# A hybrid DeltaNet/HGRN block on one core: gates and HGRN values projected token-major, head norms taken token-major

## The chip, the cores and the metric

The kernel runs as one program on one core of a Trainium2 chip. The time is device microseconds of one execution; the time before is 1231.27 us, the median of three runs (1229.66 to 1232.65). TensorE (PE) multiplies, VectorE (DVE), ScalarE (ACT) and GpSimd (POOL) do the elementwise work, SyncE (SP) and POOL issue the transfers. Each engine takes its instructions strictly in the order in which they stand in the program; which order that is, a scheduler settles when the program is built, from its own estimates of durations.

## What is computed

One layer: a normed input (256 tokens, 2048 wide) goes through one wide projection into two groups of eight heads of 128, then an output projection, a squared-ReLU feed-forward pair and a final norm, all in float32.

```
n = RMSNorm(h)
[q k v z a b | q f i g] = n @ W_in
y_A = head_norm(gated_delta(silu(conv(q, k, v)), a, b)) * silu(z)        # 8 heads, "GDN"
y_B = head_norm(hgrn2(silu(q), f, i)) * silu(g)                          # 8 heads, "HGRN"
h = h + concat(y_A, y_B) @ W_out
h = h + relu(RMSNorm(h) @ W1)^2 @ W2
out = RMSNorm(h)
```

`head_norm(o)` divides each head's 128 outputs of a token by their root mean square and multiplies by a weight of 128 entries. The delta rule inside a chunk asks for the inverse of a triangular matrix; HGRN multiplies keys and queries by exponentials of summed log gates.

## The kernel before

**Number format.** Every large float32 operand is split into two parts, `hi` (rounded, one ACT cast, L120) and `lo` (the rest, one DVE subtraction, L121), and the product is made of three terms: hi*hi, hi*lo, lo*hi. The input is stored once, transposed, as `xT`, 16 tiles k of 128 channels by 512 columns: 256 of `hi`, then 256 of `lo`.

**Projection (`project`, L286-L328).** Weights arrive as tiles `w` of 128x2048 (1 MB, SP's queue, three buffers) and are split half a tile (1024 columns) at a time into one of three buffers `hi`/`lo`. A head has four tiles: two for a pair of its outputs (chunk 0: q,k or q,f), two for the other pair (chunk 1: v,z or i,g). The weights are the stationary operand: for each k and each of the two outputs, one matmul of 512 columns (L314, hi weights against hi and lo of `xT`) and one of 256 (L315, lo weights against hi). The results lie channel-major (128 channels by 256 tokens) in a pair of PSUM banks `acc` from the pool `psA` of four, which lives as long as the kernel. ACT and DVE add the two halves into `lot`; POOL (GDN) or DVE (HGRN) multiplies by the row scale `rB`.

**Heads.** `gdn_mix` does convolutions, silu of q, k, v and z in one 1024-wide chain, norms of q and k, the two score products `pk` (L402, L403) and stores the masked scores `PA`; POOL copies their diagonal blocks to DRAM (`scr_a`). After head 7, `gdn_invert` reads the blocks back as `X`, inverts 16x16 blocks by some thirty small POOL operations (L459, L461), and sends the result round through DRAM (`scr_x`, `Xq`). `gdn_solve` builds the full inverse from `Xn` on PE (tile `pQ` first) and ends in the outputs `po`. `hgrn_mix` makes the log gates `u` (POOL adds, L600), a running sum (DVE scan, L602), the exponentials `E` (1536 wide, L614), many 32x32 products `pd` and `pa`, the matrix `A` (POOL, L663), and the output `poh` (L672, L673). The tiles `u`, `gx` and `big` (which holds `E`) have one buffer each, so the next head may overwrite them only when this head has read them. Both kinds of head end in `finish_heads` (L420-L441): squares, a sum over channels by two matmuls with ones (`pm`, L432, L433), Ln and Exp for the root, two products with the rest and the gate `SZ`, and a split into `yTa`/`yTb`, the stationary operand of the output projection.

**PSUM.** The pool `psM` has the other four banks: two for the tag `mx` (the heads' products) and two for `sv` (the solve). When the heads are done, `mctx.close()` gives its four banks back and `psB` takes them. The output projection (L782) makes its first 1024 columns in four banks of `psA`, its second in four of `psB`.

**Order.** The loop issues the projection of head n+1 before the mix of head n; the solve stands at n = 9, the inverse after n = 7. The scheduler then places the instructions on each engine, which it may move past each other where no operand forbids it: PE's row thus has matmuls of the projection, or of the output projection, between the small products of a head.

Of the kernel before, what the change touches and what calls it, by code (L numbers as in the profile page):

```python
# [15 lines left out]
P = 128  # L16
# [4 lines left out]
NH = 8  # L21
# [54 lines left out]
def hybrid_block(ctx: ExitStack, tc: tile.TileContext, x, xt, w_in, w_ab, params, w_out, w_ff1, w_ff2,  # L76
# [14 lines left out]
    psA = ctx.enter_context(tc.tile_pool(name="psA", bufs=4, space=PSUM))  # L91
# [8 lines left out]
    psM = mctx.enter_context(tc.tile_pool(name="psM", bufs=MXB, space=PSUM))  # L100

# [3 lines left out]
    def acc_a():  # L105
        return psA.tile([P, 512], F32, tag="acc", name="acc")
# [85 lines left out]

    def row_scales():
# [4 lines left out]
        PE.matmul(prb[:, 0:T], lhsT=ones, rhs=sums[:, 0:T], start=True, stop=True)  # L198
        ACT.activation(rB, prb[:, 0:T], AF.Ln, bias=eps, scale=1.0 / D)
        ACT.activation(rB, rB, AF.Exp, scale=-0.5)  # L200

    par = cpool.tile([P, 6, NH], F32, tag="par", name="par")
    lb, oml = par[:, 0, :], par[:, 1, :]
    gnw = cpool.tile([P, 2], F32, tag="gnw", name="gnw")
# [25 lines left out]
    def gates():  # L230
# [6 lines left out]
        abt = mp.tile([32, 2 * T], F32, tag="fsq2", name="abt")  # L237
# [41 lines left out]
        gr = mp.tile([NH, T], F32, tag="fsq1", name="gr")  # L279
# [3 lines left out]

    held_back = []

    def project(base, hd, chunk, dsts):  # L286
        second = base == 0 and hd == 0 and chunk == 1
        accs = [acc_a() for _ in range(2)]
        for kh in range(2):
            first = base == 0 and hd == 0 and chunk == 0  # L290
            if first:
                w = w_first[kh]
            else:
                w = wtile()
                src = w_in[((base > 0) * NH + hd) * 4 + chunk * 2 + kh]
                if second and kh == 0:
                    for c in range(4):
                        SP.dma_start(w[:, c * 512:(c + 1) * 512], src[:, c * 512:(c + 1) * 512])
                else:
                    SP.dma_start(w, src)  # L300
                if second and kh == 1:
                    SP.dma_start(cst, consts[:, 0:NKEEP])
                    SP.dma_start(cst_a, consts[:, NKEEP:])
                    SP.dma_start(wab, w_ab)
            for q in range(2):
                hi, lo = split(w[:, q * 1024:(q + 1) * 1024], 1024, pieces=2 if first or second and kh == 0 else 1)
                if second:
                    squares(2 * kh + q, lo[:, 0:1].bitcast(F32))
                hi = hi.rearrange("p (k g c) -> p k g c", k=4, g=2)
                lo = lo.rearrange("p (k g c) -> p k g c", k=4, g=2)  # L310
                for kk in range(4):
                    k = kh * 8 + q * 4 + kk
                    for g in range(2):
                        PE.matmul(accs[g], lhsT=hi[:, kk, g, :], rhs=xT[:, k, :], start=(k == 0), stop=False)  # L314
                        PE.matmul(accs[g][:, T:], lhsT=lo[:, kk, g, :], rhs=xT[:, k, 0:T],  # L315
                                  start=False, stop=(k == KT - 1))
        if second:
            row_scales()
            for lot, dst in held_back:
                POOL.tensor_tensor(out=dst, in0=lot, in1=rB, op=ALU.mult)  # L320
        for g in range(2):
            lot = mp.tile([P, T], F32, tag="lot", name="lot", bufs=2)
            ACT.copy(lot, accs[g][:, T:])
            DVE.tensor_tensor(out=lot, in0=accs[g][:, 0:T], in1=lot, op=ALU.add)
            if first:
                held_back.append((lot, dsts[g]))
            else:
                (POOL if base == 0 else DVE).tensor_tensor(out=dsts[g], in0=lot, in1=rB, op=ALU.mult)  # L328


    NRING = 12
# [7 lines left out]
    SZ = mp.tile([P, NRING, T], F32, tag="SZ", name="SZ")  # L339
# [5 lines left out]
    def gdn_project(hd):  # L345
        pre = mp.tile([P, 4, T], F32, tag="gx", name="pre").rearrange("p a t -> p (a t)")[:, 0:3 * (T + 3)]
        pre = pre.rearrange("p (a t) -> p a t", a=3)
        R = mp.tile([P, 4, T], F32, tag="R", name="R", bufs=RB)
        POOL.memset(pre[:, :, 0:3], 0.0)
        project(0, hd, 0, (pre[:, 0, 3:], pre[:, 1, 3:]))  # L350
        project(0, hd, 1, (pre[:, 2, 3:], R[:, 3, :]))
        return pre, R

    def gdn_mix(hd, pre, R):
        for i in range(3):
# [26 lines left out]
        ri = u[:, 2:4, :].rearrange("p a t -> p (a t)")  # L382
# [3 lines left out]
        DVE.tensor_tensor(out=qk, in0=qk, in1=u[:, 2:4, :], op=ALU.mult)  # L386
# [33 lines left out]
    def finish_heads(h0, nh, po, sz, scale, bank):  # L420

        n = nh * T
        if h0 >= NYA and not yTb:
            yTb[0] = ypool.tile([P, 2 * NH - NYA, 2 * T], F32R, tag="yb", name="yTb")
        sq = mp.tile([P, n], F32, tag=f"fsq{nh}", name="fsq", bufs=1)
        ACT.activation(sq, po, AF.Square)
        pm = bank("pm")[:, 0:n]
        shi = mp.tile([P, n], F32R, tag="Xn" if nh == 2 else "sh", name="shi")
        slo = mp.tile([P, n], F32R, tag="Yd" if nh == 2 else "vv", name="slo")
        ACT.copy(shi, sq)  # L430
        DVE.tensor_tensor(out=slo, in0=sq, in1=shi.bitcast(F32), op=ALU.subtract)
        PE.matmul(pm, lhsT=ones_r, rhs=shi, start=True, stop=False)  # L432
        PE.matmul(pm, lhsT=ones_r, rhs=slo, start=False, stop=True)  # L433
        ACT.activation(sq, pm, AF.Ln, bias=eps, scale=scale / P)
        ACT.activation(sq, sq, AF.Exp, scale=-0.5)
        DVE.tensor_tensor(out=sq, in0=po, in1=sq, op=ALU.mult)
        DVE.tensor_tensor(out=sq, in0=sq, in1=sz, op=ALU.mult)
        src, hs = (yTa, h0) if h0 < NYA else (yTb[0], h0 - NYA)
        yv = sq.rearrange("p (a t) -> p a t", a=nh)
        hi, lo = src[:, hs:hs + nh, 0:T], src[:, hs:hs + nh, T:]  # L440
        split(yv, None, hi, lo)  # L441
# [30 lines left out]
    def gdn_solve(Xq):  # L472
# [85 lines left out]
        for pair in range(NH // 2):  # L558
            po = sv("po")
            for n in range(2):  # L560
                hd, c = 2 * pair + n, n * T
                PE.matmul(po[:, c:c + T], lhsT=V[:, hd, 0, :], rhs=PA(hd)[:, 0, 0:T], start=True, stop=False)
                PE.matmul(po[:, c + P:c + T], lhsT=V[:, hd, 1, :], rhs=PA(hd)[:, 0, T:384], start=False, stop=True)
            finish_heads(2 * pair, 2, po, SZ[:, 2 * pair:2 * pair + 2, :].rearrange("p a t -> p (a t)"), 1.0 / P, sv)


    def hgrn_project(hd):
        R = mp.tile([P, 4, T], F32, tag="R", name="R", bufs=RB)
        project(4112, hd, 0, (R[:, 0, :], R[:, 1, :]))
        project(4112, hd, 1, (R[:, 3, :], R[:, 2, :]))  # L570
        return R

    def hgrn_mix(hd, R):

        pv = mx("pvh")
        for hf in range(2):
            PE.transpose(pv[:, hf * P:(hf + 1) * P], R[:, 3, hf * P:(hf + 1) * P], ident)
        vv = mp.tile([P, 2, P], F32, tag="vv", name="vv")
        ACT.copy(vv.rearrange("p a e -> p (a e)"), pv[:, 0:T])
        u = mp.tile([P, 4, T], F32, tag="u", name="u", bufs=UB)  # L580
        sigmoid_parts(u[:, 0:3, :], R[:, 0:3, :], 3 * T)
        DVE.scalar_tensor_tensor(out=u[:, 3, :], in0=R[:, 1, :], scalar=0.0, in1=u[:, 1, :], op0=ALU.max, op1=ALU.add)
        DVE.scalar_tensor_tensor(out=u[:, 0:3, :], in0=R[:, 0:3, :], scalar=0.0, in1=u[:, 0:3, :],
                                 op0=ALU.min, op1=ALU.subtract)
        ACT.activation(u[:, 0:3, :], u[:, 0:3, :], AF.Exp)
        ACT.activation(u[:, 3, :], u[:, 3, :], AF.Exp, scale=-1.0)
# [84 lines left out]
        po = mx("poh")[:, 0:T]  # L671
        PE.matmul(po, lhsT=vv[:, 0, :], rhs=A[:, 0:T], start=True, stop=False)  # L672
        PE.matmul(po[:, P:], lhsT=vv[:, 1, :], rhs=A[:, T:384], start=False, stop=True)  # L673
        finish_heads(NH + hd, 1, po, SZ[:, (NH + hd) % NRING, :], 1.0, mx)

    st = gdn_project(0)
    parameters()
    gates()
    for n in range(2 * NH):
        if n + 1 < 2 * NH:  # L680
            nx = gdn_project(n + 1) if n + 1 < NH else hgrn_project(n + 1 - NH)
        if n == SOLVE_AT:
            gdn_solve(Xn)
        if n < NH:
            gdn_mix(n, *st)
# [370 lines left out]
def _laid_out(i):  # L1056
# [3 lines left out]
    w = i["w_in"][0]  # L1060
# [47 lines left out]
```

## Time and profile before

| what | value |
|---|---|
| median of three runs | 1231.27 us (1229.66 to 1232.65) |
| the profiled execution, its own time | 1230.59 us |
| its span, first to last instruction | 1228.9 us |
| PE busy | 1211.9 us, 99% |
| DVE, ACT, POOL busy | 1054.7, 777.1, 136.2 us |
| first 440 us or so | projection and heads |
| about 437 to 503 us | output projection, with the last two heads in its first part |
| from about 503 us | feed-forward and final norm |

Matmuls are pipelined: a row's duration is from its start to the end of its drain, and several overlap. What a matmul costs PE in a dense stretch is the distance between two starts. The chain of work that ended last counts in these distances.

### The profile page before, as it was taken

The numbers are of one execution on the slowest core, as the hardware profiler recorded it, in microseconds if no ns is written. First come the engines' busy times: TensorE is split into PE (matmuls) and PEld (weight loads), VectorE is DVE, ScalarE is ACT, GpSimd is POOL, SyncE is SP. The second block draws the span as 40 slices with busy tenths as digits, with TensorE's granted clock in tenths as the row PEclk, the third lists the DMA queues.
The fourth block names the chain that finished last, engine by engine and source line by source line (L and its number), as shares of the span: only waits on it lengthen the run. The fifth ranks groups of instructions, "written<-read, shape, count | busy, mean of one in ns | idle before, by whom it ended". The sixth has DMA issues, their size and how long they took to land.

```text
span 1228.9 us, 18515 instructions
## 1 busy us (share of the span) xinstructions
PE 1211.9 (99%) x7058; PEld 1018.8 (83%) x7058; DVE 1054.7 (86%) x1487; ACT 777.1 (63%) x1096; POOL 136.2 (11%) x185
## 2 busy tenths in 40 slices
PE   9999999998999999999999999999999999999997
PEld 7888888887888887888888888888888888888886
DVE  7889998878789986779889889889998888989877
ACT  7667677665677765655565656566666665656653
POOL 0243433262011121000000000000000000000000
PEclk9999999998999999999999999999999999999999
DMA  9545555543336445556455545653866556556461
GB/s 337 171 149 178 182 179 188 183 161 121 127 111 233 170 169 176 211 200 234 146 203 205 210 144 195 240 199 134 324 233 214 197 177 226 186 199 215 170 232 69
DMA packets 37145, 233.46 MB, mean 190 GB/s; under 512 B 4696, under 2 KB 5728, under 8 KB 10176
## 3 DMA queue, kind: packets, MB, share of 16 engines
q1 hardware_dynamic: 34848, 229.83, 53.0%
q0 software_dynamic: 1632, 1.72, 0.9%
q8 instruction: 55, 0.90, 0.3%
q10 hardware_dynamic: 576, 0.74, 0.2%
q14 instruction: 34, 0.28, 0.1%
HBM read 227.67 MB, written 4.60 MB: 189 GB/s over the span
## 4 chain that ended last, share of the span: by engine, by line
PE 93%; POOL 2%; DVE 2%; DMA 1%; issue 1%; ACT 0%; POOLq 0%; SPq 0%; DVEq 0%
PE acc L314 17%; PE acc L812 9%; PE acc L811 9%; PE acc L813 9%; PE acc L315 9%; PE accb L811 9%; PE accb L812 9%; PE accb L813 9%; PE accb L782 4%; PE acc L782 4%; POOL X L461 1%; PE acc L823 1%; PE accb L823 1%; PE pk L402 1%; DMA X<-scr_a 1%
## 5 line engine op out<-in xcount | busy, mean ns | idle before, releaser
L121 DVE TENSOR_TENSOR lo<-w,hi 128x1024 fp32r<-128x1024 f32 (+1 forms) x422 | 487.6, 1171 | 91.5 <-ACT hi L120 81.7
L120 ACT CAST hi<-w 128x1024 fp32r<-128x1024 f32 (+1 forms) x422 | 413.2, 993 | 210.1 <-PE acc L812 55.6
L314 PE MATMUL acc<-xT,hi 128*128 128x512 f32 x1024 | 358.7, 397 | 1.1 <-ACT hi L120 1.1
L315 PE MATMUL acc<-xT,lo 128*128 128x256 f32 x1024 | 280.9, 284 | 0.3 <-DVE lo L121 0.2
L314 PEld LDWEIGHTS acc<-xT,hi 128*128 128x128 f32 x1024 | 189.3, 188 | 39.9 <-ACT hi L120 1.7
L315 PEld LDWEIGHTS acc<-xT,lo 128*128 128x128 f32 x1024 | 193.1, 189 | 7.4 <-DVE lo L121 2.1
L120 ACT CAST hi<-TT 128x1024 fp32r<-128x1024 f32 x88 | 92.0, 1052 | 77.5 <-issue 21.7
L121 DVE TENSOR_TENSOR lo<-TT,hi 128x1024 fp32r<-128x1024 f32 x88 | 106.9, 1222 | 30.3 <-ACT hi L120 27.4
L811 PE MATMUL acc<-hi,sets 128*128 128x512 f32 x260 | 101.5, 392 | 0.0
L812 PE MATMUL acc<-hi,sets 128*128 128x512 f32 x260 | 101.3, 390 | 0.0
L813 PE MATMUL acc<-lo,sets 128*128 128x512 f32 x260 | 96.1, 391 | 0.0
L811 PE MATMUL accb<-hi,sets 128*128 128x512 f32 x224 | 88.1, 393 | 0.0
L812 PE MATMUL accb<-hi,sets 128*128 128x512 f32 x224 | 87.4, 390 | 0.0
L951 POOL TENSOR_TENSOR fin<-fin,cst 128x1 f32<-128x1 f32 x2 | 1.1, 564 | 743.9 <-DVE fin L950 743.9
L813 PE MATMUL accb<-lo,sets 128*128 128x512 f32 x224 | 78.8, 392 | 0.0
L812 PE MATMUL acc<-hi,gs 128*128 128x512 f32 (+1 forms) x200 | 77.1, 385 | 0.0
L811 PE MATMUL acc<-hi,gs 128*128 128x512 f32 (+1 forms) x200 | 76.8, 386 | 0.0
L813 PE MATMUL acc<-lo,gs 128*128 128x512 f32 (+1 forms) x200 | 75.7, 386 | 0.0
L812 PE MATMUL accb<-hi,gs 128*128 128x512 f32 x188 | 73.2, 390 | 0.0
L811 PE MATMUL accb<-hi,gs 128*128 128x512 f32 x188 | 72.8, 390 | 0.0
L813 PE MATMUL accb<-lo,gs 128*128 128x512 f32 x188 | 72.6, 390 | 0.0
L851 DVE TENSOR_TENSOR TT<-w 128x1024 f32<-128x1024 f32 x44 | 53.7, 1220 | 5.9 <-DMA w<-in_w_ff_dram 5.9
(336 smaller groups left out, 2029.9 us busy)
## 6 DMA issues: line engine op xcount, KB each, us to landing
w<-in_w_ff_dram SPq DMA_DIRECT2D x128, 1024.0 KB, 5.0
w<-in_w_in_dram SPq DMA_DIRECT2D x61, 1024.0 KB, 4.9
w<-in_w_out_dram SPq DMA_DIRECT2D x16, 1024.0 KB, 4.9
w<-in_w_in_dram SPq DMA_DIRECT2D x12, 256.0 KB, 5.4
big<-in_xt_dram SPq DMA_DIRECT2D x8, 256.0 KB, 5.5
h<-in_x_dram SPq DMA_DIRECT2D x2, 1024.0 KB, 5.9
scr_h<-h SPq DMA_DIRECT2D x4, 512.0 KB, 5.1
tail<-scr_h SPq DMA_DIRECT2D x2, 1024.0 KB, 6.4
```

The lines of the kernel that those rows point to most:

```text
L120: ACT.copy(hi, w)
L121: eng.tensor_tensor(out=lo, in0=w, in1=hi.bitcast(F32), op=ALU.subtract)
L314: PE.matmul(accs[g], lhsT=hi[:, kk, g, :], rhs=xT[:, k, :], start=(k == 0), stop=False)
L315: PE.matmul(accs[g][:, T:], lhsT=lo[:, kk, g, :], rhs=xT[:, k, 0:T], start=False, stop=(k == KT - 1))
L402: PE.matmul(pk0, lhsT=R[:, 1, 0:P], rhs=qk.rearrange("p a t -> p (a t)"), start=True, stop=True)
L461: POOL.tensor_tensor(out=X[:, j + 1:, 0:ncol], in0=X[:, j + 1:, 0:ncol], in1=t3, op=ALU.subtract)
L782: PE.matmul(accs[2 * hf + c], lhsT=st, rhs=ww[:, c * 512:(c + 1) * 512], start=(k == 0 and a == 0 and ww is hi), stop=(k == 2 * NH - 1 and ...
L811: PE.matmul(dst, lhsT=ah, rhs=bh, start=start, stop=False)
L812: PE.matmul(dst, lhsT=al, rhs=bh, start=False, stop=False)
L813: PE.matmul(dst, lhsT=ah, rhs=bl, start=False, stop=stop)
L823: PE.transpose(pt[:, c * P:(c + 1) * P], src[:, c * P:(c + 1) * P], ident)
L851: DVE.tensor_tensor(out=TT[:, 0:1024].rearrange("p (a c) -> p a c", a=2), in0=view(w, 0, [[1536, 2], [1, 512]]), in1=view(w, 512, [[-512, ...
```

## The change

- **Tiles.** A GDN head now has a pair of tiles for q,k, one tile with all 16 k of v alone, and one tile with four k of a group of 512 z columns (four heads). An HGRN head has its pair q,f and two tiles with four k each of a group of 512 columns, i and g of two heads. All heads still have four tiles of 128x2048; only the host's layout of `w_in` changes what is in them.
- **Token-major products (`project_tokens`).** For z, i and g the input is the stationary operand and the weights stream: for each k and each half of the tokens, three matmuls of 512 columns into one of two banks `tok`. These banks add up over four GDN heads or two HGRN heads. `tokens_out` then takes them to SBUF with a per-token scale `rcol` (made by two extra one-column matmuls in `row_scales`), and `silu` runs over 512 columns at a time. The tile `R` has three parts instead of four and GDN heads allocate it in the mix.
- **HGRN values.** i comes out token-major, so the two transposes `pvh` and the copy `vv` go.
- **Head norms (`finish_heads`).** Outputs `po`/`poh` are made token-major (three 128-column products). ACT squares each 128x128 block and sums it along the row (`accum_out`) into `ss`; Ln and Exp run on two or four columns; DVE multiplies output, root and gate in one instruction per block, in place in the gate's tile; PE transposes the blocks (`pt`, L487 in the new file); ACT and DVE split the result, with the norm weight `gnw` as scale. The two matmuls with ones go. The squares of the two kinds of heads have scratch tiles of their own.
- **PSUM.** `psA` is no longer there during the heads. The pool `psM` takes banks 0 to 3 and a new `psP` banks 4 to 7 (two `acc`, two `tok`); v accumulates in an `sv` bank. After `mctx.close()`, `psA` is opened first and gets banks 0 to 3, then `psB` with 4 to 7.

The core of the diff:

```
-    psA = ctx.enter_context(tc.tile_pool(name="psA", bufs=4, space=PSUM))
...
+    psP = mctx.enter_context(tc.tile_pool(name="psP", bufs=2, space=PSUM))
...
+    def project_tokens(c):
+        if c == 0:
+            tok[0] = [acc_p("tok") for _ in range(2)]
+        accs = tok[0]
+        w, n = w_next()
+        for q, hi, lo in halves_of(w, n):
+            for kk in range(2):
+                k = c * 4 + q * 2 + kk
+                cs = slice(kk * 512, (kk + 1) * 512)
+                for hf in range(2):
+                    for a, ww in ((0, hi), (T, hi), (0, lo)):
+                        PE.matmul(accs[hf], lhsT=xT[:, k, a + hf * P:a + hf * P + P], rhs=ww[:, cs],
+                                  start=(k == 0 and a == 0 and ww is hi), stop=(k == KT - 1 and ww is lo))
...
+    def tokens_out(dst):
+        for hf in range(2):
+            ACT.activation(dst[:, hf, :], tok[0][hf], AF.Copy, scale=rcol[:, hf:hf + 1])
...
+        project((pre[:, 0, 3:], pre[:, 1, 3:]), POOL, lambda: acc_p("acc"))
+        project((pre[:, 2, 3:],), POOL, lambda: sv("accv"))
+        project_tokens(hd % 4)
+        if hd % 4 == 3:
+            tokens_out(SZ[:, hd // 4])
+            for hf in range(2):
+                silu(SZ[:, hd // 4, hf])
...
+        for hf, n, c in at:
+            ACT.activation(sq, po[:, hf, c], AF.Square, accum_out=ss[:, hf, n:n + 1])
+        ACT.activation(ss, ss, AF.Ln, bias=eps, scale=scale / P)
+        ACT.activation(ss, ss, AF.Exp, scale=-0.5)
+        for hf, n, c in at:
+            DVE.scalar_tensor_tensor(out=sz[:, hf, c], in0=po[:, hf, c], scalar=ss[:, hf, n:n + 1], in1=sz[:, hf, c],
+                                     op0=ALU.mult, op1=ALU.mult)
+        pt = bank("pt")[:, 0:nh * T]
+        for hf, n, c in at:
+            PE.transpose(pt[:, n * T + hf * P:n * T + hf * P + P], sz[:, hf, c], ident)
...
     mctx.close()
+    psA = ctx.enter_context(tc.tile_pool(name="psA", bufs=4, space=PSUM))
     psB = ctx.enter_context(tc.tile_pool(name="psB", bufs=4, space=PSUM))
```

The first place is PE's row where the input projection ends. Before, its last matmuls (L314, L315) are followed at once by the output projection (L782), and the last head's products stand among it; these are pieces of that stretch, the second from the last head.

```order
L314 MATMUL acc<-xT,hi 128x512
L315 MATMUL acc<-xT,lo 128x256
L782 MATMUL acc<-hi,yTa 128x512 x4
L782 MATMUL acc<-lo,yTa 128x512 x2
L577 MATMUL pvh<-cst,R 128x128 x2
...
L638 MATMUL pd<-E 32x32 x32
L653 MATMUL pa<-L 128x128
L782 MATMUL acc<-lo,yTa 128x512 x3
...
L672 MATMUL poh<-A,vv 128x256
L782 MATMUL acc<-hi,yTb 128x512 x3
```

In the changed program, from the last token-major matmul (L358) on; `pd`, `pa`, `poh`, `pt` of HGRN head 6 and then of head 7:

```order
L358 MATMUL acc<-hi,xT 128x512 x2
L358 MATMUL acc<-lo,xT 128x512
L693 MATMUL pd<-E 32x32 x28
L708 MATMUL pa<-L 128x128
L727 MATMUL poh<-ig,A 128x128
L487 MATMUL pt<-cst,ig 128x128 x2
L693 MATMUL pd<-E 32x32 x32
L708 MATMUL pa<-L 128x128
L727 MATMUL poh<-ig,A 128x128
L487 MATMUL pt<-cst,ig 128x128 x2
L845 MATMUL acc<-hi,yTa 128x512 x4
```

The output projection (L845) has moved behind the last head: no large matmul stands between the products of heads 6 and 7, and the first one stands after the last head's transposes.

The second place is POOL's row at the inverse. Before, `A` of HGRN head 8 (the first one, L663) stands inside the chain of small operations on `X`:

```order
L459 TENSOR_TENSOR Xt<-X 128x55
L663 TENSOR_TENSOR A<-rd,cst_a 128x128 x2
L461 TENSOR_TENSOR X<-X,Xt 128x5x11
...
L462 AFFINE_SELECT X<-X 128x256
L465 DMA scr_x<-X 64x256 x2
L468 DMA Xq<-scr_x 64x16x16 x2
L498 MEMSET XP 64x1024
L600 TENSOR_TENSOR u<-u 128x256
```

In the changed program the same operations on POOL, from the chain's last ones on:

```order
L511 TENSOR_TENSOR Xt<-X 128x15
L513 TENSOR_TENSOR X<-X,Xt 128x15
L514 AFFINE_SELECT X<-X 128x256
L517 DMA scr_x<-X 64x256 x2
L718 TENSOR_TENSOR A<-rd,cst_a 128x128 x2
L655 TENSOR_TENSOR u<-u 128x256
L520 DMA Xq<-scr_x 64x16x16 x2
```

`A` of that head has moved behind the whole chain and behind the issue of its transfer.

More of the change, by code (lines that the diff above doesn't have):

```diff
@@ L278, in gates @@
             PE.matmul(pr[0:NH, hf * P:(hf + 1) * P], lhsT=gate[:, hf, 0:NH], rhs=C("upper"), start=True, stop=True)
-        gr = mp.tile([NH, T], F32, tag="fsq1", name="gr")
+        gr = mp.tile([NH, T], F32, tag="A", name="gr")
         ACT.copy(gr, pr[0:NH, 0:T])
         POOL.dma_start(scr_g, gr)
+    tiles = [0]
     held_back = []
[L286 to L313, printed above, removed]
@@ new lines, in w_next @@
+    def w_next():
+        n = tiles[0]
+        tiles[0] += 1
+        if n < 2:
+            return w_first[n], n
+        w = wtile()
+        if n == 2:
+            for c in range(4):
+                SP.dma_start(w[:, c * 512:(c + 1) * 512], w_in[n][:, c * 512:(c + 1) * 512])
+        else:
+            SP.dma_start(w, w_in[n])
+        if n == 3:
+            SP.dma_start(cst, consts[:, 0:NKEEP])
+            SP.dma_start(cst_a, consts[:, NKEEP:])
+            SP.dma_start(wab, w_ab)
+        return w, n
@@ new lines, in halves_of, with project @@
+    def halves_of(w, n):
+        for q in range(2):
+            hi, lo = split(w[:, q * 1024:(q + 1) * 1024], 1024, pieces=2 if n < 3 else 1)
+            if n in (2, 3):
+                squares(2 * (n - 2) + q, lo[:, 0:1].bitcast(F32))
+            yield q, hi, lo
+    def project(dsts, eng, bank):
+        ng = len(dsts)
+        accs = [bank() for _ in range(ng)]
+        for kh in range(ng):
+            w, n = w_next()
+            for q, hi, lo in halves_of(w, n):
+                hi = hi.rearrange("p (k g c) -> p k g c", g=ng, c=P)
+                lo = lo.rearrange("p (k g c) -> p k g c", g=ng, c=P)
+                for kk in range(8 // ng):
+                    k = (2 * kh + q) * (8 // ng) + kk
+                    for g in range(ng):
@@ L316, in project @@
                                   start=False, stop=(k == KT - 1))
[L317 to L321, printed above, removed]
+        for g in range(ng):
             lot = mp.tile([P, T], F32, tag="lot", name="lot", bufs=2)
             ACT.copy(lot, accs[g][:, T:])
-            DVE.tensor_tensor(out=lot, in0=accs[g][:, 0:T], in1=lot, op=ALU.add)
-            if first:
-                held_back.append((lot, dsts[g]))
-            else:
-                (POOL if base == 0 else DVE).tensor_tensor(out=dsts[g], in0=lot, in1=rB, op=ALU.mult)
@@ L418, in yT, with finish_heads @@
         return yTa[:, k, a:b] if k < NYA else yTb[0][:, k - NYA, a:b]
-    def finish_heads(h0, nh, po, sz, scale, bank):
-        n = nh * T
+    def finish_heads(h0, nh, po, sz, group, scale, bank):
         if h0 >= NYA and not yTb:
             yTb[0] = ypool.tile([P, 2 * NH - NYA, 2 * T], F32R, tag="yb", name="yTb")
[L425 to L437, printed above, removed]
+        ss = mp.tile([P, 2, nh], F32, tag=f"ss{nh}", name="ss")
+        sq = mp.tile([P, P], F32, tag=f"fsq{nh}", name="fsq")
+        at = [(hf, n, slice(n * P, (n + 1) * P)) for hf in range(2) for n in range(nh)]
+        for hf, n, c in at:
[8 more added lines that the diff above has]
+            PE.transpose(pt[:, n * T + hf * P:n * T + hf * P + P], sz[:, hf, c], ident)
@@ L438, in finish_heads @@
         src, hs = (yTa, h0) if h0 < NYA else (yTb[0], h0 - NYA)
[L439 removed]
+        pt = pt.rearrange("p (a t) -> p a t", a=nh)
         hi, lo = src[:, hs:hs + nh, 0:T], src[:, hs:hs + nh, T:]
[L441 removed]
+        ACT.activation(hi, pt, AF.Copy, scale=gnw[:, group:group + 1])
+        DVE.scalar_tensor_tensor(out=lo, in0=pt, scalar=gnw[:, group:group + 1], in1=hi.bitcast(F32), op0=ALU.mult,
+                                 op1=ALU.subtract)
@@ new lines, in gdn_solve @@
+            finish_heads(2 * pair, 2, po, SZ[:, pair // 2, :, pair % 2 * T:pair % 2 * T + T], 0, 1.0 / P, sv)
+    ig = [None]
+    def hgrn_project(hd):
+        R = mp.tile([P, 3, T], F32, tag="R", name="R", bufs=RB)
+        project((R[:, 0, :], R[:, 1, :]), DVE, lambda: acc_p("acc"))
+        for c in range(2):
+            project_tokens(hd % 2 * 2 + c)
+        if hd % 2 == 1:
+            ig[0] = mp.tile([P, 2, 512], F32, tag="ig", name="ig", bufs=2)
+            tokens_out(ig[0])
+            silu(ig[0][:, :, T:])
@@ L571, in hgrn_project @@
         return R
     def hgrn_mix(hd, R):
[L575 to L582, printed above, removed]
```

117 lines of the change are left out of this document (77 added, 40 removed).

## The prediction

> **What bounds the kernel now.** First the page: span and busy time of each engine.
>
> ```profile
> span 1228.9 us, 18515 instructions
> PE 1211.9 (99%) x7058; PEld 1018.8 (83%) x7058; DVE 1054.7 (86%) x1487; ACT 777.1 (63%) x1096; POOL 136.2 (11%) x185
> ```
>
> PE is busy for 1211.9 of 1228.9 us. So two things count: the work that the change takes from PE or gives it, and every place where it makes PE wait. The table of waits, for PE, lists its waits of today: engine, line, what it waited for, total, times, longest.
>
> ```profile
> PE accb L782 <- DVE fsq L436: 2.0, 1, 2.0
> PE pd L638 <- issue: 1.9, 1, 1.9
> PE poh L672 <- POOL Xt L459: 1.1, 1, 1.1
> PE pP L513 <- DVE Xn L492: 0.9, 1, 0.9
> PE pQ L484 <- DVE Xn L477: 0.2, 1, 0.2
> ```
>
> They are few, and they lie at two places: four about the inverse, and one, the longest, where the output projection changes from `acc` to `accb`. That one is telling: `accb` are the banks of `psB`, which were `psM`'s, and their first product waits until DVE has read the last head's `poh` (L436). The half before it, in `psA`, waits for nobody. The table of windows of PE, at that place (stretch, its length, PE busy, instructions, granted clock, DMA share, GB/s):
>
> ```profile
> 484.00:488.00 4.00, 1.96 (x10) 1.00 0.28 119
> 488.00:492.00 4.00, 4.00 (x13) 0.63 0.71 262
> ```
>
> After the wait of 2.0 us the granted clock is 0.63 over 4 us: some 1.5 us more are lost (4.0 x 0.37).
>
> **PE's own work.** The price of a matmul in a dense stretch is the distance between starts. The timeline of PE, in the middle of a projection, and the chain of waits, in the output projection and the last head (start, us, what, count):
>
> ```profile
> 149.76 0.39 PE L314 MATMUL acc<-xT,hi 128*128 128x512 f32 x1
> ...
> 151.49 0.63 PE L314 MATMUL acc<-xT,hi 128*128 128x512 f32 x2
> ```
>
> ```profile
> 469.99 0.22 PE pvh L577 x2
> ...
> 473.89 0.66 PE pd L638 x49
> ...
> 475.71 6.39 PE acc L782 x28
> 482.10 0.43 PE poh L672 x2
> 482.53 0.22 PE poh L673 x2
> ...
> 503.47 34.05 PE accb L782 x150
> ```
>
> Five pairs (one of 512 columns, one of 256) take 151.49-149.76 = 1.73 us, 0.346 each. A stream of 512 alone, with a new stationary operand each time as the token-major products have it, takes 34.05/150 = 0.227. So 256 columns cost 0.346-0.227 = 0.119, and 128 cost 0.22/2 = 0.11.
> - Per k of a group of 512 outputs the old form is four pairs, 1.384 us, the new one six streams, 1.362. There are 96 such (16 k; two groups of z, four of i and g): -2.1 us.
> - The sums over channels go: `pm`, 8 products of 512 (-1.8) and 16 of 256 (-1.9). `pvh` goes: 16 x 0.11 = -1.8. `pt` comes: 32 x 0.11 = +3.5.
> - The outputs `po`, `poh` keep their columns (two products of 256 and two of 128, 0.65 us, become six of 128, 0.66): nothing. Two one-column products for `rcol`, bounds 0 and 2 x 0.11: +0.2.
>
> Sum -3.9 us. Bounds: -2, if the new form gains nothing on the old one (without the 2.1), and -6, if two thirds of `pt` run in gaps that PE has anyway.
>
> The Trainium skill, page "TensorE: Matmul & The Clock Gate", section "Wait — 56ns, not 53.3ns?", gives a warm matmul N / 2.4 GHz plus about 2.5 ns. By it, an estimate, the token-major form would save only 0.5 us (1.300 against 1.295 us per k). The trace has 227 and 346 ns, and I go by these; the sum moves by 1.6 us.
>
> ACT and DVE lose work on balance (DVE's half of the squares and products, the copies `vv`), POOL loses the rescaling of half its `R`; the squares now taken on ACT, at most 32 of 0.39 us (the old 256-wide square, quoted below), lie beside PE's projection. I cost these at nothing, because DVE is idle 14% and ACT 37% of the span; where the cover of PE's work is gone, they are counted in the next part. SP's order of loads is unchanged.
>
> **The end of the heads.** Here the order shows the large move. In the changed program `psA` is opened first after `mctx.close()`, gets banks 0 to 3, and those are `psM`'s: `mx` and `sv` of the last heads. By the row of waits above, such a reopened bank waits for the last head. PE is in order, so with L845 behind head 7's `pt` nothing large covers heads 6 and 7; before, the `psA` half did. The question is how long the bare chain is. Its rows, from head 7 of before (timelines of DVE, POOL, ACT):
>
> ```profile
> 459.71 0.68 DVE L602 TENSOR_TENSOR_SCAN gx<-cst_a,u 128x256 f32<-128x256 f32 x1
> 461.43 2.19 DVE L608 TENSOR_TENSOR E<-gx 128x256 f32<-128x256 f32 x5 [1.05 <-POOL gx L603]
> 466.15 1.76 DVE L623 TENSOR_TENSOR E<-E,gx 128x256 f32<-128x256 f32 x5
> 467.83 0.69 DVE L624 TENSOR_TENSOR E<-E,gx 128x512 f32<-128x512 f32 x1
> 469.90 0.41 DVE L627 TENSOR_TENSOR L<-E,ec 128x256 f32<-128x256 f32 x1
> 472.49 1.23 DVE L121 TENSOR_TENSOR lo<-w,hi 128x1024 fp32r<-128x1024 f32 x1 [0.71 <-ACT hi L120]
> 474.85 0.57 DVE L656 TENSOR_TENSOR pd<-pd,cst_a 128x384 f32<-128x384 f32 x1 [0.79 <-PE pd L641]
> 475.45 0.56 DVE L660 TENSOR_REDUCE rd<-pd 128x64 f32<-128x384 f32 x1
> ```
>
> ```profile
> 458.25 1.25 POOL L600 TENSOR_TENSOR u<-u 128x256 f32<-128x256 f32 x1 [5.08 <-ACT u L599]
> 460.55 0.85 POOL L603 TENSOR_SCALAR gx<-gx 128x256 f32<-128x256 f32 x1 [1.04 <-PE acc L782]
> 476.15 1.83 POOL L663 TENSOR_TENSOR A<-rd,cst_a 128x128 f32<-128x128 f32 x2 [13.81 <-DVE rd L660]
> ```
>
> ```profile
> 463.72 1.49 ACT L614 ACTIVATE E<-E 128x1536 f32<-128x1536 f32 x1
> 478.01 0.26 ACT L667 COPY A<-pa 64x128 f32<-64x128 f32 x1 [2.00 <-POOL A L663]
> 478.18 0.41 ACT L670 COPY A<-pa 32x64 f32<-32x64 f32 x2
> 482.79 0.39 ACT L426 ACTIVATE fsq<-poh 128x256 f32<-128x256 f32 x1 [0.28 <-PE poh L673]
> 485.82 0.47 ACT L434 ACTIVATE fsq<-pm,cst 128x256 f32<-128x256 f32 x1
> 486.32 0.42 ACT L435 ACTIVATE fsq<-fsq 128x256 f32<-128x256 f32 x1
> ```
>
> Clock at 0 when the last matmul of the input projection is done; each step by its row:
> - head 6: small products 473.89 to 475.71, 1.8; one `lo` of the output weights still in DVE's way, 1.2; mask and sum 0.57+0.56; `A` on POOL 1.8. At 6.0.
> - head 7: POOL's `u`, which stands behind that `A`, 1.25; scan 0.7; negation 0.85; differences 2.2; exponentials 1.5; products 1.8+0.7; `L` 0.4 and head 6's split of the same size 0.4. At 15.8. (`u`, `gx`, `big` have one buffer, and POOL's order holds it besides: that is why head 7 doesn't start sooner.)
> - head 7's small products were PE's between them except the last, its mask and sum 1.1, `A` 1.8, copies 0.7, `poh` 0.65, at 20.0; squares 2 x 0.39, Ln and Exp 0.9 at most (their rows are 256 wide, the new ones two), the product with the gate 0.4, `pt` 0.2, split 0.8. At 23.2; with nineteen handovers of about 0.04 us it is 24.
>
> In these 24 us PE has 2 x 1.8 (small products) + 2 x 0.65 + 2 x 0.22 = 5.4 us of its own work, which it would do anyway: 18.6 idle. The wait of before, 2.0, goes; the 1.5 of half clock behind it stay. Small products at a lower clock add about 0.5. Net **+17 us**, bounds +10 (squares, Ln, `A` overlap better, `u` of head 7 earlier) and +21 (more splits of weights in DVE's and ACT's way; before, with them, this chain took 458.25 to 486.74 for head 7 alone, 28.5).
>
> **The inverse.** The chain from the last `pk` to the first `pQ` goes through DRAM and thirty operations of POOL and does not depend on PE (chain of waits; timelines of DVE and POOL):
>
> ```profile
> 237.73 0.86 PE pk L402 x2
> ```
>
> ```profile
> 267.94 0.76 POOL L663 TENSOR_TENSOR A<-rd,cst_a 128x128 f32<-128x128 f32 x2
> ...
> 273.71 1.14 POOL L465 DMA_DIRECT2D scr_x<-X  x2 [0.29 <-POOL X L462]
> ```
>
> ```profile
> 284.50 0.97 DVE Xn L477 x2
> ```
>
> It takes 285.5-237.7 = 47.7 us. Between `pk` and `pQ` the order has 117 pairs of the projection before (117 x 0.346 = 40.5 us), and 64 pairs and 50 token-major streams now (22.1+11.4 = 33.5): PE's cover is 7.0 us less, because the last `pk` has moved behind work that stood after it. `pvh` and `pm` go from there, 0.7 less. `A` of head 8, now behind the chain, makes the chain 0.8 shorter. So the stall there, 1.1+0.2 us now, grows by 7.0+0.7-0.8 = **+7**, the most of it at head 8's `poh`, which waits for that `A` and through it for the whole chain until the issue at 273.71. Bounds 0 (if the last `pk` really comes as early on the clock as before) and +10 (with 1.5 to 3 of lowered clock behind it).
>
> The same page, section "What's actually happening", says that PE's clock is halved after an idle window of about 3.4 us. The rows here agree (0.63 behind a wait of 2.0 us); by the rule both new stalls pay it, an estimate of 1.7 us each, which lies within the bounds.
>
> **Sum.** -3.9 + 17 + 7 = +20. The profiled execution took 1230.59 us of its own (1.7 around the span), 0.7 below the median of 1231.27. So 1230.6 + 20 + 0.7 = **1251 us**.
>
> **Rivals.**
> 1. The end of the heads is hidden after all (faster). Then only PE's work counts, and the wait of 2.0 and its clock, 1.5, go too: -3.9-3.5, 1224 us. The price is the bare chain; it decides at about 5.4+3.9+2.0 = 11 us, below which the change gains even with `psA` behind the last head (and the inverse as before). Against it: POOL's `A` twice and the exponentials' chain of head 7 alone come to 13.3 us, and the order forbids cover. 4%.
> 2. A short handover (the +10) with the inverse as before: +6, 1237 us. For it: the chain from `pk` might be met by other work. 10%.
> 3. The inverse costs ten more, because `poh` and `pQ` both wait and PE's half clock, seen there already, spreads: 1261 us. For it:
>
> ```profile
> 296.00:299.00 3.00, 2.86 (x88) 0.50 0.76 311
> ```
>
> PE ran at half clock just behind today's short waits at this place. 10%.
> 4. That the even load does nothing: the heads had four tiles each before too, so it is not counted as a gain at all.
>
> **How the numbers follow.** Forecast 76%: 1251, its own bounds 1230.6+0.7-6+10+0 = 1235 and 1230.6+0.7-2+21+10 = 1260. The range 1236 to 1261 leaves out rival 1, half of rival 2 and the ends. About 0.2% (2.5 us) can be told from no change here. Faster by more: rival 1, 0.04. Within it: the lowest end of rival 2, 0.02. Slower: 0.94.
>
> **What would show it.** Right: in the profile after, PE idle for 15 to 20 us in several pieces just ahead of the first L845, with waits on DVE, POOL and ACT of heads 6 and 7; granted clock about 0.5 in that stretch; L358 at distances of 0.227; a wait of `poh` (L727) on POOL of 4 us or more near the inverse. Wrong: PE's idle time ahead of L845 below 8 us, or L845 that starts at a distance from the projection's end of less than 15 us; an inverse whose waits stay near 1 us; distances of L358 nearer 0.25 (0.023 x 576 = 13 us more), which would mean that streaming weights is dearer beside three buffers than in the output projection.

## The result, and the profile after

The changed kernel takes 1248.8 us, the median of four runs (1247.89 to 1253.12), against 1231.59 (four runs, 1229.66 to 1232.65): 1.0148 of the time before, 95% interval 1.0121 to 1.0175, so 17 us more. The forecast was 1251, in a range of 1236 to 1261. The profiled execution took 1249.3 us.

The page of the changed kernel, span and busy times:

```profile
span 1247.6 us, 18180 instructions
PE 1215.6 (97%) x6894; PEld 1013.8 (81%) x6894; DVE 1033.4 (83%) x1443; ACT 776.8 (62%) x1150; POOL 118.9 (10%) x177
```

PE was idle 17 us before (1228.9-1211.9) and is now idle 32; the rest of the loss is time at a lowered clock (the granted clock of the profile, as a share of full speed), in which PE counts as busy. The table of waits for PE (what it waited for; us in total, times, longest):

```profile
PE poh L727 <- POOL u L655: 7.3, 2, 4.2
PE pt L487 <- DVE ig L483: 5.5, 3, 3.0
PE pQ L542 <- issue: 3.5, 1, 3.5
...
PE pd L693 <- DVE E L678: 1.4, 1, 1.4
PE poh L727 <- POOL A L718: 1.2, 1, 1.2
PE acc L845 <- DVE yTb L492: 1.1, 1, 1.1
```

The old wait of `accb` is gone, and six new ones stand at the end of the heads (of the 7.3 us of `poh` 4.18 are there, of the 5.5 of `pt` 4.96; the others are at the inverse). The timeline of PE there, from the end of the projection to the first product of the output projection (start, us, engine, line, what; in brackets the wait ahead of it):

```profile
442.20 0.66 PE L693 MATMUL pd<-E 128*32 128x32 f32 x54
...
448.21 0.77 PE L727 MATMUL poh<-ig,A 128*128 128x128 f32 x2 [4.18 <-POOL u L655]
...
452.84 0.66 PE L487 MATMUL pt<-cst,ig 128*128 128x128 f32 x2 [3.01 <-DVE ig L483]
454.95 1.35 PE L693 MATMUL pd<-E 128*32 128x32 f32 x64 [1.45 <-DVE E L678]
...
459.83 0.76 PE L727 MATMUL poh<-ig,A 128*128 128x128 f32 x2 [1.20 <-POOL A L718]
...
463.40 0.66 PE L487 MATMUL pt<-cst,ig 128*128 128x128 f32 x2 [1.95 <-DVE ig L483]
465.14 2.08 PE L845 MATMUL acc<-hi,yTa 128*128 128x512 f32 x4 [1.08 <-DVE yTb L492]
```

From 442.2 to 465.14 is 22.9 us; the forecast's bare chain was 24. No large product stands in it. The windows of PE give the clock there (stretch, length, PE busy, granted clock, DMA share, GB/s):

```profile
442.00:446.00 4.00, 2.03 (x88) 1.00 0.76 260
446.00:450.00 4.00, 1.62 (x6) 0.75 0.01 2
450.00:454.00 4.00, 0.66 (x2) 0.50 0.02 4
454.00:458.00 4.00, 2.92 (x93) 0.50 0.00 0
458.00:462.00 4.00, 2.25 (x8) 0.50 0.00 0
462.00:466.00 4.00, 1.51 (x4) 0.50 0.02 6
466.00:470.00 4.00, 4.00 (x14) 0.69 0.00 0
470.00:474.00 4.00, 4.00 (x19) 1.00 0.34 80
```

The clock is whole while the first small products run, falls in the first wait, and stays at half to the end of the chain, even in a window where PE is 73% busy. Dense work begins at 465.14; if the 0.69 of the window from 466 is time at half and time at full speed, the clock came back at about 468.5, some 3 us later.

To compare kernels I use one measure, worked out from the timeline of PE: the **lost time**, the sum over PE's matmuls of the distance to the next start beyond the median distance for that line and number of columns in the same run (a shorter distance counts against it). It counts waits and lowered clock alike. By stretches of the span, in us:

| kernel | 30 to 230 | 230 to 330 (inverse) | 330 to 430 | 430 to 475 | 475 to 500 | whole span |
|---|---|---|---|---|---|---|
| before | 1.9 | 12.0 | 2.3 | 0.9 | 4.2 | 23.1 |
| changed | 3.3 | 15.6 | 1.5 | 19.8 | 0.0 | 42.5 |
| psB first | 2.9 | 16.3 | 2.4 | 1.6 | 0.1 | 24.8 |
| psB first, R early | 3.2 | 15.2 | 3.5 | 1.3 | 0.1 | 25.4 |
| before, psA reopened | 3.2 | 10.6 | 1.0 | 27.6 | 1.0 | 45.8 |
| psB first, solve at 10 | 2.9 | 9.9 | 5.6 | 1.7 | 0.1 | 22.0 |
| psB first, solve at 10, A on DVE | 2.9 | 9.0 | 4.1 | 1.3 | 0.0 | 18.7 |

Where half of a group of small products ran at half clock, its median is itself too high. With the medians of psB first, the row of the changed kernel reads 3.0, 17.4, 2.4, 20.4, 0.0 and 45.3: some 3 us are hidden, most of them at the inverse.

### The profile page after: what moved, and what is told of

Its sections match the earlier page's. It is cut to its first block, busy times and chain, and to the rows that moved or that the text cites. A ratio compares the mean times of both kernels' runs of the same rounds, so it can differ in the third digit from the quotient of the medians.

```text
span 1247.6 us, 18180 instructions
## 1 busy us (share of the span) xinstructions
PE 1215.6 (97%) x6894; PEld 1013.8 (81%) x6894; DVE 1033.4 (83%) x1443; ACT 776.8 (62%) x1150; POOL 118.9 (10%) x177
## 4 chain that ended last, share of the span: by engine, by line
PE 92%; POOL 2%; issue 2%; DMA 2%; DVE 1%; ACT 1%; SPq 0%; POOLq 0%; DVEq 0%; ACTq 0%
PE acc L358 10%; PE acc L875 9%; PE acc L876 9%; PE acc L874 9%; PE accb L875 8%; PE accb L874 8%; PE accb L876 8%; PE acc L331 8%; PE acc L332 4%; PE acc L845 4%; PE accb L845 3%; PE accv L331 2%; PE accv L332 1%; POOL X L513 1%; PE acc L886 1%
## 5 line engine op out<-in xcount | busy, mean ns | idle before, releaser
L331 PE MATMUL acc<-xT,hi 128*128 128x512 f32 x512 | 180.6, 399 | 1.7 <-ACT hi L120 1.7
L332 PE MATMUL acc<-xT,lo 128*128 128x256 f32 x512 | 140.4, 285 | 0.0
L358 PE MATMUL acc<-hi,xT 128*128 128x512 f32 x384 | 119.1, 398 | 0.0
L331 PEld LDWEIGHTS acc<-xT,hi 128*128 128x128 f32 x512 | 94.9, 189 | 21.6 <-ACT hi L120 2.2
L332 PEld LDWEIGHTS acc<-xT,lo 128*128 128x128 f32 x512 | 96.7, 190 | 4.5 <-DVE lo L121 1.2
L358 PEld LDWEIGHTS acc<-hi,xT 128*128 128x128 f32 x384 | 71.9, 191 | 14.9
L358 PE MATMUL acc<-lo,xT 128*128 128x512 f32 x192 | 73.5, 399 | 0.0
L875 PE MATMUL accb<-hi,gs 128*128 128x512 f32 x188 | 73.1, 389 | 0.0
```

The lines of the kernel that those rows point to most:

```text
L358: PE.matmul(accs[hf], lhsT=xT[:, k, a + hf * P:a + hf * P + P], rhs=ww[:, cs], start=(k == 0 and a == 0 and ww is hi), stop=(k == KT - 1 a ...
L875: PE.matmul(dst, lhsT=al, rhs=bh, start=False, stop=False)
```

## The experiments

My theory, A: the time is lost because the reopened `psA` lies in the banks of the last heads, so that nothing covers heads 6 and 7 (cover: large products that PE has to do meanwhile); less is lost at the inverse, where the last `pk` comes later; PE's own work falls by 4 us. The rivals: B, the new head norms are slow wherever the banks lie, or a late `pk` costs nothing; and C, D and E on what holds PE at the inverse, stated with their runs.

**psB ahead of psA.**

```
-    psA = ctx.enter_context(tc.tile_pool(name="psA", bufs=4, space=PSUM))
     psB = ctx.enter_context(tc.tile_pool(name="psB", bufs=4, space=PSUM))
+    psA = ctx.enter_context(tc.tile_pool(name="psA", bufs=4, space=PSUM))
```

> The changed kernel with one thing other: psB is opened ahead of psA, so that the first half of the output projection lies in banks 4 to 7, which the projection leaves, and not in those of the last heads. Theory A (the time at the end of the heads is the cover taken away by the banks' order, 23 us from the last L358 to the first L845 of which before paid about 4): the six waits of the products of heads 6 and 7 go, one wait of about 2 us comes back where accb begins, and the time falls by 13 to 17 us, to 1232 to 1236. Theory B (the new head norms on ACT and DVE make the last heads slow, whatever the banks): PE still waits 10 us or more for yTb, and the time falls by less than 5 us.

Measured: 1228.4 us, 0.9988 of before (0.9978 to 0.9998). Two lines exchanged take 20 us off the changed kernel, more than theory A asked, because not even the old wait at `accb` comes back. All of its waits of PE:

```profile
PE poh L727 <- POOL u L655: 2.8, 1, 2.8
PE pQ L542 <- issue: 2.1, 1, 2.1
PE pt L487 <- DVE ig L483: 1.9, 1, 1.9
PE pP L565 <- issue: 1.4, 1, 1.4
PE warm L175 <- POOL pre L396: 1.0, 1, 1.0
PE acc L331 <- ACT hi L120: 0.6, 1, 0.6
```

They are all at the inverse and the start. The chain of work that ended last shows why none stands at the change of banks: the last head's transposes are done 10 us before the first product of `accb`.

```profile
480.29 0.22 PE pt L487 x2
480.51 9.80 PE acc L845 x43
490.31 4.31 PE accb L845 x19
```

Theory B on the norms is out.

**The counter-test: before, with psA reopened.** The heads of the kernel before get an `acc` pool of their own behind `psM`, and `psA` is opened anew, first, when they are done.

```
-    psA = ctx.enter_context(tc.tile_pool(name="psA", bufs=4, space=PSUM))
...
     psM = mctx.enter_context(tc.tile_pool(name="psM", bufs=MXB, space=PSUM))
+    psP = mctx.enter_context(tc.tile_pool(name="psP", bufs=4, space=PSUM))
...
     mctx.close()
+    psA = ctx.enter_context(tc.tile_pool(name="psA", bufs=4, space=PSUM))
     psB = ctx.enter_context(tc.tile_pool(name="psB", bufs=4, space=PSUM))
```

> The kernel before with one thing other: the heads' acc banks are a pool psP opened behind psM and closed with the heads, and psA is opened ahead of psB afterwards, so that the first half of the output projection lies in psM's banks. Nothing is token-major. Theory A (banks' order alone): the output projection falls behind the last head, and the time rises by 12 to 20 us, to 1244 to 1251. Theory B (the new head norms make the bare chain): under 8 us.

Measured: 1256.49 us, 1.0211 (1.0198 to 1.0224), 26 us more; above theory A's 12 to 20. Its timeline of PE:

```profile
440.14 0.38 PE L579 MATMUL pvh<-cst,R 128*128 128x128 f32 x2
445.69 0.44 PE L640 MATMUL pd<-E 128*32 128x32 f32 x16 [5.17 <-DVE E L625]
...
462.09 0.44 PE L640 MATMUL pd<-E 128*32 128x32 f32 x16 [5.69 <-DVE E L625]
...
471.74 2.08 PE L786 MATMUL acc<-hi,yTa 128*128 128x512 f32 x4 [1.47 <-DVE fsq L438]
```

The bare chain of the old heads takes 471.7-440.1 = 31.6 us, that of the new ones 22.9. So the banks' order alone is enough for the damage. Of the 8.7 us between the two chains, 5.5 lie ahead of head 6's first `pd`, whose `E` isn't ready when the old projection ends; from there on they take 26.1 and 22.9 us. How much of that the new form of the heads saves, and how much the other order, these runs don't separate.

**R taken early.** The change had a side effect: z used to be written to R in `gdn_project`, and so R had its buffer before the next head's. A write of one column gives that back.

```
     def gdn_project(hd):
+        R = mp.tile([P, 3, T], F32, tag="R", name="R", bufs=RB)
...
+        POOL.memset(R[:, 0, 0:1], 0.0)
```

> The changed kernel with one thing other: a GDN head's R is taken in gdn_project, by a write of one column, and not in the mix, as it was in effect before the change (z was written to it there). In the order the last pk then comes after 202 us of large products and not 220, pQ has 39.9 us of cover and not 33.4, and POOL's A of HGRN head 0 stands in the chain again. Theory A (the stalls at the inverse are cover lost because R of head 7 waits for head 6's): PE's waits between 250 and 325 us fall from 15 us to about 11, and the time by 4 to 7 us, to 1242 to 1245. Theory B (a late pk costs nothing, the stall there is the short products' own): within 1.5 us of the changed kernel.

Measured: 1251.22 us, 1.0171 (1.0158 to 1.0185): not faster than the changed kernel. With psB first as well:

> The changed kernel with both edits: psB ahead of psA, and R taken in gdn_project. Theory A: what is left of the change is PE's own work, 3 to 4 us less than before, and perhaps 1 us of waits: 1226 to 1231, faster than the kernel before by 1 to 5 us. Theory B (something else in the change, such as token-major streams or transposes, costs as well): slower than the kernel before, 1233 or more.

Measured: 1231.57 us, 1.0008 (0.9999 to 1.0016), within 0.2% of before, and 3 us slower than psB first alone. So theory A fell on the inverse: 6.5 us more cover behind the last `pk` bought nothing. What `poh` of HGRN head 0 waits for has moved, not gone:

```profile
PE poh L729 <- POOL X L516: 3.6, 1, 3.6
```

**A of HGRN head 0 on DVE.** If that wait, through POOL, is what is left, A has to leave POOL. One edit in three kernels:

```
-            POOL.tensor_tensor(out=A[:, t * T:t * T + P].rearrange("p (b c) -> p b c", b=4),
+            (DVE if hd == 0 else POOL).tensor_tensor(out=A[:, t * T:t * T + P].rearrange("p (b c) -> p b c", b=4),
```

With psB first:

> The changed kernel with psB ahead of psA and, beside that, A of HGRN head 0 alone made on DVE and not on POOL, so that it doesn't stand behind the inversion's chain. Theory C (what is left at the inverse is poh of that head, which waits through POOL for the whole chain, and the lowered clock behind it): the wait of poh of 2.8 us goes, and the time falls below that of the run with psB ahead alone (1228.4) by 3 to 5 us, to 1223.5 to 1225.5. Theory D (the chain through DRAM ends when it ends, and PE waits at pQ instead, so that the sum of the stalls there stays near 16 us): 1227.5 to 1229.5.

Measured: 1229.74 us, 0.9992 (0.9979 to 1.0005): no gain, as D has it, if 0.2 above its range. With psB first and R early:

> As the run with psB ahead and R taken in gdn_project, and A of HGRN head 0 on DVE. Theory C: the wait of poh of 3.6 us goes, the time falls from 1231.6 by 3 to 5 us, to 1226.5 to 1228.5. Theory D: the stall moves to pQ, whose cover in the order is now 35.4 us behind the last pk and was 39.9: 1231 to 1235.

Measured: 1230.74 us, 0.9999 (0.9989 to 1.0008): neither's range quite, nearer D. In the kernel before:

> The kernel before with A of HGRN head 0 on DVE and nothing else. Its poh waits 1.3 us for POOL there. Theory C: 1 to 2 us faster than before, 1229 to 1230. Theory D: pQ's cover falls from 40.6 to 37.5 us in the order, so PE waits there: 0 to 3 us slower, 1231 to 1234.

Measured: 1241.72 us, 1.0086 (1.0073 to 1.0099): slower by 10 us, on D's side and far beyond its size. In this run PE waits 5.7 us for `E` at `pd` and 4.1 for `Xn` at `pQ`. In each of the three `poh`'s wait is gone and another has come. The second one shows how; DVE's timeline, then PE's:

```profile
269.93 0.69 DVE L659 TENSOR_TENSOR_SCAN gx<-cst_a,u 128x256 f32<-128x256 f32 x1 [5.57 <-POOL u L657]
```

```profile
271.80 0.50 PE L358 MATMUL acc<-lo,xT 128*128 128x512 f32 x1 [2.93 <-DVE lo L121]
```

The next head's `u` stands on POOL behind the inversion's chain as well. DVE reaches that head's scan and stops for 5.6 us; the split of weights (`lo`) stands behind the scan, and now PE waits 2.9 us for that. The profiled execution of the first run (1236.59 us, 7 above the median) shows the same path, with waits of 11.51 and 6.40 us; but there one POOL operation of the inversion (L511) took 7.73 us, 0.84 in the changed kernel, so its lengths say nothing of a usual execution.

**The solve one head later**, with psB first:

```
-SOLVE_AT, INVERT_AT = 9, 7
+SOLVE_AT, INVERT_AT = 10, 7
```

> The changed kernel with psB ahead of psA, and with the solve one head later in the program (SOLVE_AT 10 for 9), which gives the first pQ 37.1 us of cover behind the last pk and had 33.4, and takes small products of the solve from between those of the HGRN heads. Theory D (the stalls at the inverse are the wait for the end of the chain through DRAM, cover counts): PE's waits between 230 and 330 us fall from 16 us to about 12, and the time from 1228.4 to 1224 to 1226. Theory E (they are the solve's and heads' small products themselves, at lowered clock and each behind a step on DVE or ACT, whenever the solve comes): within 1.5 us of 1228.4.

Measured: 1228.93 us, 0.9986 (0.9976 to 0.9996), the same as psB first alone. D was right that the lost time at the inverse falls (16.3 to 9.9 us), E that the time of the kernel doesn't: half of it comes back in the next stretch (2.4 to 5.6), and the profiled execution (1226.85 us) was 2 us below the median of its runs. With A of head 0 on DVE besides:

> The changed kernel with psB ahead of psA, SOLVE_AT 10, and A of HGRN head 0 on DVE. If the stalls at the inverse add up (poh's wait 2.6 us, pQ's gone with the later solve), both go: PE's waits between 230 and 330 us fall from 9.9 us to 6 or less, and the time to 1223 to 1226. If what is saved at one place is paid at the next, as the runs so far had it: 1228 to 1231.

Measured: 1225.31 us, 0.9952 (0.9940 to 0.9965): the fastest of all, 5.6 us below before. The time is the one expected if the stalls add up; the lost time at the inverse fell less than that (9.9 to 9.0, where 6 or less was expected), and its profiled execution (1222.4 us) is the shortest of its six. Its granted clock over 230 to 330 us was 1.00, against 0.95 with psB first alone and 0.98 with the solve at 10. Its longest waits of PE (the second is at the start of the kernel):

```profile
PE acc L358 <- DVE lo L121: 1.4, 1, 1.4
PE warm L175 <- POOL pre L396: 1.0, 1, 1.0
```

With R early in place of A on DVE:

> The changed kernel with psB ahead of psA, SOLVE_AT 10, and R taken in gdn_project. The order has 54.6 us of cover between the last pk and the first pQ, more than the 48 us that the chain between them took with R taken there. If cover of that chain counts: no wait at pQ, poh's of 3.6 us alone left, 1224 to 1227. If the early pk gives nothing, as with SOLVE_AT 9: 1229 to 1232.

Measured: 1228.78 us, 0.9980 (0.9971 to 0.9988). Even 54.6 us of cover behind the last `pk` changes nothing; `poh` waits 3.3 us.

**One scratch tile of squares.** The part of the change to which I had given no thought at all, undone in the changed kernel:

```
-        sq = mp.tile([P, P], F32, tag=f"fsq{nh}", name="fsq")
+        sq = mp.tile([P, P], F32, tag="fsq", name="fsq")
```

> The changed kernel with one part of the change undone: one scratch tile of squares for both kinds of heads. The squares' result is read by nobody and ACT makes them in order, so theory A expects no wait from it: within 2 us of the changed kernel's 1248.8. Rival: the shared tile ties the solve's heads to the HGRN heads in the scheduler's plan, and the time rises by 3 us or more.

Measured: 1274.46 us, 1.0346 (1.0333 to 1.0360): 26 us slower than the changed kernel. The rival is right. On ACT's row in the order, all squares of the solve's heads (`po`) now stand ahead of the squares of HGRN head 1, since the one buffer is handed on in the program's order; that head waits for the solve (its squares begin at 388.2 us, 321.1 in the changed kernel), and four heads instead of two have their products behind the projection's end (four `poh`, from 441.3 to 482.0). The windows of PE, first with the shared tile:

```profile
430.00:500.00 70.00, 38.76 (x477) 0.63 0.14 46
```

and in the changed kernel:

```profile
430.00:500.00 70.00, 57.00 (x405) 0.85 0.37 122
```

And with psB first, where 40.9 us of large products stand among those late heads:

> The changed kernel with psB ahead of psA, and with the one scratch tile of squares for both kinds of heads. In the order three HGRN heads and not two then follow the end of the input projection, but with 40.9 us of the output projection's first half among them. Theory A (late heads cost only what nothing covers): of the 26 us that the shared tile cost beside the changed kernel at most 5 are left, 1228 to 1234. Rival (a shared tile costs by the waits on ACT and DVE themselves, with cover or without): 1245 or more.

Measured: 1246.02 us, 1.0118 (1.0103 to 1.0134), 18 us slower than psB first with two tiles. My number fell, and the rival's (1245 or more) was met. The waits are again those of heads without cover, now the last two (these are head 6's), once the first half (192 x 0.227 = 43.6 us) is nearly spent:

```profile
487.21 0.46 PE L727 MATMUL poh<-ig,A 128*128 128x128 f32 x2 [1.21 <-POOL u L655]
...
491.64 0.66 PE L487 MATMUL pt<-cst,ig 128*128 128x128 f32 x2 [3.52 <-DVE ig L483]
493.22 2.07 PE L845 MATMUL acc<-hi,yTb 128*128 128x512 f32 x4 [0.93 <-ACT yTb L491]
```

Of the 16.6 us of lost time that this kernel has beyond psB first (41.4 against 24.8 over the whole span), 14.4 lie between 475 and 520 us, behind the cover and not all along, as waits on ACT and DVE by themselves would. Cover delays the loss; it does not do away with a chain that is longer than the cover.

## Why the prediction was right, and where it was not

**PE's own work, -3.9: right.** The run with psB first has the same matmuls as the changed kernel and little lost time. From PE's first start to its last it takes 1217.4 us, of which 24.8 are lost; before, 1219.4 and 23.1. That is 1192.6 against 1196.3, -3.7. A token-major stream costs what the output projection's did; from the chain of work that ended last in the changed kernel, 5.47/24 = 0.228 us each:

```profile
24.87 5.47 PE acc L358 x24
```

**The end of the heads, +17: right in place, near in sum.** The exchange of the pools takes 20.4 us off the changed kernel (1248.8 to 1228.4). Of that, 0.9+4.2-1.6-0.1 = 3.4 us are lost time that the kernel before still had there, so the change's own cost is 17.0 by difference. By the lost time at the place itself it is less: 19.8-0.9-4.2 = 14.7, or 15.3 with the medians of psB first. By its terms: the chain of 22.9 us against 24; idle PE in it 4.18+3.01+1.45+1.20+1.95+1.08 = 12.9 us, where I had 18.6; and PE's own 5.4 us of work took 10.0, most of it at half clock, where I had allowed 0.5 more. Two errors of 4 to 6 us, of opposite sign, and that they nearly cancel is luck: I had taken the clock as lost mainly behind the chain, and it was lost from the first wait on. The Trainium skill, page "TensorE: Matmul & The Clock Gate", section "What's actually happening", has the clock fall after an idle window of about 3.4 us; here it fell at the wait of 4.18 us, in agreement. The prediction has the kernel before agree too, which is not so: its wait was 2.0 us, shorter than that window, and the clock fell behind it all the same (0.63).

**The inverse, +7: right in sign, too large, and for a wrong reason.** The sum leaves 17.2+3.7-17.0 = 3.9 us for it and all the rest (5.6 with the 15.3), and the lost time there rose by 3.6 (12.0 to 15.6; by 5.4 with the medians of psB first). The wait of `poh` behind the chain came, but was smaller than forecast (3.1 us, forecast 4 or more). The step that failed is "the chain is 0.8 shorter": I had carried the rest of its 47.7 us over. PE, POOL and DVE in the changed kernel:

```profile
252.50 1.02 PE L453 MATMUL pk<-R 128*128 128x512 f32 x2
```

```profile
261.17 1.66 POOL L501 DMA_DIRECT2D X<-scr_a  x2 [2.60 <-DMA scr_a<-PA]
...
267.28 0.51 POOL L505 TENSOR_SCALAR_AFFINE_SELECT X<-X 128x256 f32<-128x256 f32 x1 [1.82 <-DMA X<-scr_a]
...
284.90 1.16 POOL L517 DMA_DIRECT2D scr_x<-X  x2 [0.30 <-POOL X L514]
286.05 0.79 POOL L718 TENSOR_TENSOR A<-rd,cst_a 128x128 f32<-128x128 f32 x2
...
287.99 1.71 POOL L520 DMA_DIRECT2D Xq<-scr_x  x2 [0.48 <-issue]
```

```profile
293.06 0.62 DVE L529 TENSOR_SCALAR Xn<-Xq,cst_a 128x256 f32<-128x256 f32 x2 [1.84 <-DMA Xq<-scr_x]
```

and POOL before:

```profile
245.44 1.19 POOL L600 TENSOR_TENSOR u<-u 128x256 f32<-128x256 f32 x1 [2.95 <-ACT u L599]
248.35 1.71 POOL L449 DMA_DIRECT2D X<-scr_a  x2
...
278.85 1.68 POOL L468 DMA_DIRECT2D Xq<-scr_x  x2 [4.01 <-DMA scr_x<-X]
```

With the last `pk` at 252.5, `Xn` is ready at 293.7, 41.2 us on, not 47. The thirty operations on `X`, with `A` taken from among them, are no shorter: from the first of them to the issue of `scr_x` they take 17.6 us in both kernels (256.10 to 273.71; 267.28 to 284.90). What is shorter lies around them. The next head's `u`, which stands on POOL ahead of the read of `X`, no longer holds it up (before, it waited 2.95 us there, and the read was issued 10.6 us behind `pk`, 248.35-237.73; now 8.7). That isn't owed to the later `pk` alone: with psB first and R early it comes at 235.05, and the read is issued 7.1 us behind it. The read's data come sooner, 6.1 us after its issue against 7.8, and `Xq` is issued 3.1 us after `scr_x` against 5.1; why these two are shorter no run shows. So the first `pQ` waits for nothing, and the cover that I counted as lost was not needed. The run with psB first and R early shows from the other side that the chain's length isn't fixed: cover came back (39.9 us), and the chain took 48.4 us again (235.05 to 283.45), with `A` back in it, `Xq` issued 5.7 us after `scr_x`, and `Xn` begun 9.1 us after that issue, against 5.1 in the changed kernel. PE's order, POOL's order and the chain were made by one scheduler, and moved together.

**What I had not costed.** The separate scratch tiles: I let them pass as nothing. They are no gain over before, which had no such tie, but without them the changed kernel would have been 26 us slower still.

**The signs named.** The granted clock of 0.50 at the place and the 0.228 us of L358 came as said. PE's idle time ahead of L845 (12.9 us, where 15 to 20 were said) and the wait of `poh` at the inverse (3.1, where 4 or more were said) fell short, but not so far as what would have counted as wrong.

**The rivals.** That the end of the heads is hidden (1224) didn't come; its price holds, though: with psB first it is hidden, and 1228.4 less the 3.9 us at the inverse is 1224.5. Rivals 2 and 3 didn't come either: the end of the heads cost 15 us or more and not 10, the inverse some 4 to 5 more and not 17.

**Open.** Why the lost time at the inverse is 4 to 5 us higher with the change is not settled. PE's listed waits there are 7.7 us against 4.3: 3.1 against 1.1 at `poh`, and 4.0 against 1.9 without a releaser in the profile ("issue", below). The granted clock over 230 to 330 us is 0.93 against 0.97. Taking R early or A on DVE moved the lost time without removing it; with the solve at 10 it fell below that of before (9.9 against 12.0), but half of that came back in the next stretch. The profile supports that POOL's chain holds up everything of the HGRN heads that stands behind it on POOL, but no run took the chain itself off POOL.

## What to carry to other kernels

When pools of PSUM are closed and reopened, ask which banks each new pool gets, who read them last, and what was to run meanwhile: the first user of a bank waits for its last reader, and on an engine in order all that stands behind waits too. A scratch tile that nobody reads can still tie two independent chains together by its buffer, in the program's order. And a stall at the end of a long chain is not its length minus a fixed cover: an edit that moves the start of the chain moves its queueing too, so take the chain's length anew from the new order, row by row.

## What the runs showed of the hardware

A granted clock of 0.50 held for 16 us in which PE was busy 17% to 73% of each window of 4 us with small products; it came back only when dense large products ran. And PE's wait of 3.55 us within one group of 128 equal products of `pQ` has no releaser in the profile:

```profile
300.11 1.14 PE L542 MATMUL pQ<-Pm,Yd 32*32 32x16 f32 x115
304.80 0.40 PE L542 MATMUL pQ<-Pm,Yd 32*32 32x16 f32 x13 [3.55 <-issue]
```

The same kind of wait ("issue") stood there before the change (1.9 us at `pd`) and in most runs (2.1 us with psB first, 0.6 in the fastest), mostly among the smallest products; in the kernel before with psA reopened one of 2.6 us stands at `poh`. What it is, these runs don't tell.
